# Start addresses of TensorE's operands in SBUF: all tiles moved to multiples of 256 bytes

## The chip, the cores and the metric

The kernel runs on one core of a Trainium2 chip. The metric is device time in microseconds for one execution. Three runs of the kernel before gave 1081.52, 1080.88 and 1080.98 us; the median is 1080.98.

## The reference

One layer of a hybrid decoder: a sequence of 1024 tokens of width 1024, one projection into 6672 columns, two mixers side by side (stick-breaking attention with 16 heads of 64, and a Mamba-2 scan with 16 heads of 64 in chunks of 128), one output projection, a residual with a gate, and a final norm. Everything is in fp32.

```python
mod = silu(c) @ w_ada + b_ada
shift, scale, gate = split(mod, 3)
h = rms_norm(x, norm_in_gain) * (1 + scale) + shift
q, k, v, z_attn, xbc, dt_raw, z_ssm = split(h @ w_in, splits)
o = stick_breaking_attention(q, k, v)
y_attn = rms_norm(o, sb_norm_gain) * silu(z_attn)
xbc = silu(causal_depthwise_conv(xbc, conv_w, conv_b))
y = ssd_scan(xs, softplus(dt_raw + dt_bias), -exp(a_log), b_ssm, c_ssm, d_skip)
y_ssm = rms_norm(y * silu(z_ssm), ssm_norm_gain)
x = x + gate * (concatenate([y_attn, y_ssm]) @ w_out)
return rms_norm(x, norm_f_gain)
```

## The kernel before

**Split products.** A product in fp32 is made of three matmuls in the format fp32r. An operand is split into a high part (hi, the value rounded to fp32r) and a low part (lo, what is left), and hi by hi, hi by lo and lo by hi are added in PSUM; lo by lo is dropped. The normed and modulated input h is kept, transposed, as eight pairs of tiles hh0 to hh7 (hi) and hl0 to hl7 (lo) of 128 x 1024. A piece of w_in is loaded into a raw tile; ScalarE or VectorE makes whi from it, and VectorE subtracts to make wlo (the function split). Most other matmuls (transposes, the values of the attention, the scan) are plain fp32.

A matmul has a stationary operand of 128 x 128, here called the weights, which is loaded ahead of it (LDWEIGHTS, engine PEld in the profile), and a moving operand that is streamed through, here of 512, 384, 272, 256 or 128 columns. In a group of the profile such as pj<-hh,whi the moving tile comes first, the weights second.

**The lines of the split products.** L278 (in mm_f) is the projection with 512 moving columns of hh or hl and the weights whi, wlo: 39 jobs of 48 matmuls. L517 is the same for the first four column blocks, in the first stage. L323, L324 and L327 make the values and dt: there a slice of h is the weights, and whi or wlo are the moving tile, 256 or 272 columns wide. L944 makes the attention scores from q and k. L1101 and L1112 are one more projection job cut in another order. L1047 is the output projection: the weights come from the mixers' results, which are loaded again and split like a piece of w_in, and the moving tile is w_out in hi and lo (woh, wol, and big, bc and be for the second half). L1369 is its last job, with a first part of 512 columns and then two of 256.

**Stages.** Until about 60 us the loads of x, w_ada and the first weights, the modulation, and the first projections (L517). Then the values (L323 and following), the rest of the convolution's columns (L278), the scan (L763 to L777) with projections woven in, and from about 200 us the attention, eight pairs of heads: scores (L944), transposes of the weights (L997), values (L1009), each time with a share of further projections (L278) in between to fill TensorE. After 860 us comes the output projection (L1047), at the end of it alone on TensorE. A table of costs and due times in the code decides at record time what goes between what; from the attention on, the order on each engine is written out by hand.

**Where tiles lie.** SBUF has one address range in each partition; a tile takes the same bytes in all 128. Pools stand one behind the other, in the order in which they are opened: cp (constants), hp (hh and hl), wp (raw, whi, wlo), sp (everything else). In a pool, tiles stand in the order in which their tags are first asked for. Each is padded to 32 bytes. A raw, whi or wlo tile has 544 columns, 2176 bytes, which is 8.5 times 256, so that neighbours differ by 128 in their place within 256 bytes; most others are 4096 or 8192 bytes. The tags raw (two tiles), whi and wlo (four each) are handed out in turn. Every fifth split of the later stages goes to two tiles of tag st instead.

```python
def wtile(dtype, tag):
    return mk(wp, tag, [P, 544], dtype, bufs={"raw": 2, "whi": 4, "wlo": 4}[tag])
```

Of the kernel before, what the change touches and what calls it, by code (L numbers as in the profile page):

```python
# [8 lines left out]
F32 = mybir.dt.float32  # L9
F32R = mybir.dt.float32r  # L10
# [4 lines left out]
P = 128  # L15
S = 1024
D = 1024
KT = 8
TB = 8
HALF = 512  # L20
# [6 lines left out]
def hybrid_layer_kernel(  # L27
# [40 lines left out]
    hp = ctx.enter_context(tc.tile_pool(name="hp", bufs=1))  # L68
    wp = ctx.enter_context(tc.tile_pool(name="wp", bufs=2))
    sp = ctx.enter_context(tc.tile_pool(name="sp", bufs=2))  # L70
    dr = ctx.enter_context(tc.tile_pool(name="dr", bufs=1, space=bass.MemoryType.DRAM))
    pj = ctx.enter_context(tc.tile_pool(name="pj", bufs=2, space=bass.MemoryType.PSUM))
    pz = ctx.enter_context(tc.tile_pool(name="pz", bufs=4, space=bass.MemoryType.PSUM))
# [5 lines left out]
    def mk(pool, tag, shape, dtype=F32, bufs=None):  # L79
        uid[0] += 1  # L80
        kw = {} if bufs is None else {"bufs": bufs}
        return pool.tile(shape, dtype, tag=tag, name=f"{tag}_{uid[0]}", **kw)

    def const(name, shape, dtype=F32):
        return cp.tile(shape, dtype, tag=name, name=name)
# [4 lines left out]
    def duo(dtype=F32):  # L90
        return mk(sp, "be", [P, 2, S], dtype, bufs=4)
# [2 lines left out]
        return mk(pool, tag, [P, HALF])  # L94


    rows = mk(sp, "cbm", [P, 2, P], bufs=2)[:, 0, :]
    pinned[0] = True
    A.dma_start(rows[0:8, :], c.rearrange("o (k p) -> (o k) p", p=P))
# [3 lines left out]
    make_identity(nc, ident)  # L103
    ones = const("ones", [P, P])
    G.memset(ones, 1.0)
    eps_t = const("eps_t", [P, 2])
    G.memset(eps_t[:, 0:1], EPS)
    G.memset(eps_t[:, 1:2], 4.0 * EPS)
    pr = bank(pv, "pv")
# [5 lines left out]
    V.scalar_tensor_tensor(cact, cact, 1.0, cols[:, 0:8], op0=ALU.add, op1=ALU.mult)  # L115
    V.tensor_scalar_mul(cact, cact, 0.5)

    tri = const("tri", [P, P])
    G.affine_select(out=tri, in_=ones, compare_op=ALU.is_ge, fill=0.0, base=0,
                    pattern=[[1, P]], channel_multiplier=-1)  # L120
    late_at = {}
# [57 lines left out]

    h_hi, h_lo = [None] * KT, [None] * KT  # L180

    def wtile(dtype, tag):
        return mk(wp, tag, [P, 544], dtype, bufs={"raw": 2, "whi": 4, "wlo": 4}[tag])

    def split(raw, n, room=None):

        hi, lo = room or (wtile(F32R, "whi")[:, :n], wtile(F32R, "wlo")[:, :n])
        if pinned[0]:
            V.tensor_copy(hi, raw[:, :n])
        else:  # L190
            A.copy(hi, raw[:, :n])
        V.tensor_tensor(lo, raw[:, :n], hi.bitcast(F32), op=ALU.subtract)
        return hi, lo
# [12 lines left out]

    def load_piece(piece, tag="raw"):
        kind, a, g = piece[0], piece[1], piece[2]
        raw = wtile(F32, tag)
        if kind == "f":  # L210
            src = w_in[0][g * HALF:(g + 1) * HALF, a:a + P].rearrange("(k p) f -> p k f", p=P)
            SP.dma_start(raw[:, :HALF].rearrange("p (k f) -> p k f", f=P), src)
        elif kind == "v":
            src = w_in[0][2 * g * P:2 * (g + 1) * P, C_V + a * 256:C_V + (a + 1) * 256]
            SP.dma_start(raw[:, :HALF].rearrange("p (k f) -> p k f", f=256),
                         src.rearrange("(k p) f -> p k f", p=P))
        elif kind == "g":
            SP.dma_start(raw[:, :HALF], w_ada[0][a * P:(a + 1) * P, 2048 + g * HALF:2048 + (g + 1) * HALF])
        elif kind == "b":
            SP.dma_start(raw[0:1, :HALF], b_ada[:, 2048 + g * HALF:2048 + (g + 1) * HALF])  # L220
        else:
            assert piece[3] is u_d or stored == set(range(8))
            src = piece[3][4 * g:4 * g + 4, :, a * P:(a + 1) * P]
            SP.dma_start(raw[:, :HALF].rearrange("p (k t) -> p k t", t=P), src.rearrange("k p t -> p k t"))
        return raw[:, :HALF]
# [72 lines left out]
    def inproj_v(vc, with_dt, v_tiles, dt_raw, extra=None):  # L298

        n = 272 if with_dt else 256  # L300
        wts = {}
        if not with_dt:
            for q, (whi, wlo) in enumerate(take(4)):
                for k in range(2):
                    wts[2 * q + k] = (whi, wlo, slice(k * n, (k + 1) * n))
        else:
            for k0 in range(0, KT, 2):
                raw = wtile(F32, "raw")
                rv = raw[:, :2 * n].rearrange("p (k f) -> p k f", f=n)
                rs = slice(k0 * P, (k0 + 2) * P)  # L310
                SP.dma_start(rv[:, :, :256], w_in[0][rs, C_V + vc * 256:C_V + (vc + 1) * 256]
                             .rearrange("(k p) f -> p k f", p=P))
                SP.dma_start(rv[:, :, 256:272], w_in[0][rs, C_DT:C_DT + 16]
                             .rearrange("(k p) f -> p k f", p=P))
                whi, wlo = split(raw, 2 * n)
                for k in range(2):
                    wts[k0 + k] = (whi, wlo, slice(k * n, (k + 1) * n))
        for i in range(TB):
            ps = bank(pj, "pj")
            ts_ = slice(i * P, (i + 1) * P)  # L320
            for k in range(KT):
                whi, wlo, ws = wts[k]
                K(T.matmul(ps[:, :n], h_hi[k][:, ts_], whi[:, ws], start=(k == 0), stop=False))  # L323
                K(T.matmul(ps[:, :n], h_hi[k][:, ts_], wlo[:, ws], start=False, stop=False))  # L324
                if i == 0 and extra:
                    extra(ps[:, n:n + TB], k)
                K(T.matmul(ps[:, :n], h_lo[k][:, ts_], whi[:, ws], start=False, stop=(k == KT - 1)))  # L327
                if not with_dt:
                    ahead()
                    if i == TB - 1 and k % 2:  # L330
                        used()
                if k == 3:
                    yield 1.4
            if i == 0 and extra:
                extra(ps[:, n:n + TB], KT)
            for j in range(2):
                A.copy(v_tiles[j][:, i * P:(i + 1) * P], ps[:, j * P:(j + 1) * P])
            if with_dt:
                A.copy(dt_raw[:, i, :], ps[:, 256:272])
            yield 1.4  # L340
# [4 lines left out]

    xt = [None] * TB
    ssq = const("ssq", [P, TB])
    rstd = const("rstd", [P, TB])
    shc = const("shc", [P, 8])
    gsc = const("gsc", [P, 8])  # L350
    cact32 = mk(sp, "st", [P, 8, 32], bufs=2)
    V.memset(cact32, 0.0)
    V.tensor_copy(cact32[:, :, 0:1], cact.unsqueeze(2))
# [32 lines left out]

    def load_w4(k):
        if k >= 6:
            w_raw[k] = wtile(F32, "raw")[:, :HALF]
        else:  # L390
            if k % 2 == 0:
                spare.append(mk(sp, "v", [P, 2, HALF], bufs=3))
            w_raw[k] = spare[-1][:, k % 2]
        SP.dma_start(w_raw[k], w_in[0][k * P:(k + 1) * P, C_XBC:C_XBC + HALF])
# [2 lines left out]

    def split_w4(k):
        if k < 4:
            w_hi[k], w_lo[k] = wtile(F32R, "whi")[:, :HALF], wtile(F32R, "wlo")[:, :HALF]  # L400
        else:
            if k == 4:
                w_far["lo"] = duo(F32R)
            if k % 2 == 0:
                w_far["hi"] = mk(sp, "sq", [P, 2, HALF], F32R, bufs=2)
            w_hi[k] = w_far["hi"][:, k % 2]
            w_lo[k] = w_far["lo"][:, k // 2 % 2, k % 2 * HALF:(k % 2 + 1) * HALF]
        A.copy(w_hi[k], w_raw[k])
# [20 lines left out]
    A.activation(rstd[:, 0:1], eps_t[:, 0:1], AF.Sqrt)  # L429

    def norm_x(i):
        junk = mk(sp, "om", [P, 1028], bufs=2)
        A.activation(junk[:, :S], xt[i], AF.Square, accum_out=ssq[:, i:i + 1])
        A.activation(rstd[:, i:i + 1], ssq[:, i:i + 1], AF.Sqrt, scale=1.0 / D, bias=eps_t[:, 0:1])
        V.reciprocal(rstd[:, i:i + 1], rstd[:, i:i + 1])
        V.tensor_scalar_mul(xt[i], xt[i], rstd[:, i:i + 1])
# [88 lines left out]
        A.copy(u[:, 3 + b * HALF:3 + (b + 1) * HALF], ps)  # L525

    def conv_buf(wide=False):
        u = duo().rearrange("p u s -> p (u s)") if wide else mk(sp, "om", [P, 1028], bufs=2)
        G.memset(u[:, 0:3], 0.0)
        return u  # L530

# [49 lines left out]
    for c_ in range(1, 4):  # L581
        k = 2 * c_ - 2
# [129 lines left out]
    def ssd_group(g):  # L712
# [12 lines left out]
        for ch in range(TB):  # L725
# [26 lines left out]
            V.tensor_tensor(xd[:, 0], px.rearrange("p (h r) -> p h r", r=64),  # L752
                            dt_t[:, ch, hs].unsqueeze(2).broadcast_to([P, 8, 64]), op=ALU.mult)
            py = bank(pz, "pz")
            cd = mk(sp, "cdy", [P, 8], bufs=2)
            V.tensor_copy(cd, abc[:, :, P - 1])
            if ch > 0:
                V.tensor_tensor(abc, abc, Ct[:, ts_].unsqueeze(1).broadcast_to([P, 8, P]), op=ALU.mult)
# [46 lines left out]
    def gated(j):  # L805
        if not pinned[0]:
            if j == 0:
                A.activation(sq_s, xs[j], AF.Square)
            else:
                sq = mk(sp, "om", [P, 1028], bufs=2)[:, :S]  # L810
                A.activation(sq, xs[j], AF.Square)
                V.tensor_tensor(sq_s, sq_s, sq, op=ALU.add)
            A.activation(xs[j], xs[j], AF.Copy, scale=cols[:, 100 + j:101 + j])
            SP.dma_start(u_d[j], xs[j])
            return
# [110 lines left out]
    def scores(p, g):  # L926
# [5 lines left out]
        for i in {i for i, _, _ in GROUPS[g]}:  # L932
            if i % 2 == 1:
                tiles[p, i // 2] = [duo(), duo()]
        oms = [mk(sp, "om", [P, 1028], bufs=2), mk(sp, "bc", [P, S], bufs=4)]
        parts = []
        for i, c0, cw_ in GROUPS[g]:
            zs = [bank(pz, "pz") for _ in range(2)]
# [383 lines left out]
    fs = const("fs", [P, TB])  # L1322

    def load_t2(i):
        t2 = mk(sp, "om", [P, 1028], bufs=2)[:, :S]
        SP.dma_start(t2, t2_d[i])
        return t2

# [5 lines left out]
    for i in range(TB):  # L1334
        t2 = t2s[i]
# [21 lines left out]
            after(3.0, finish)  # L1357
            continue

        part = const("part", [P, 3])  # L1360
        yt = take(2)
        cuts = ((0, 512), (512, 768), (768, 1024))
        for n, (c0, c1) in enumerate(cuts):
# [56 lines left out]
```

## Time and profile before

| what | value |
|---|---|
| median of three runs | 1080.98 us |
| the profiled execution | 1080.97 us |
| its span, first to last instruction | 1079.2 us |
| mean granted TensorE clock | 0.999 |
| DVE busy | 767.2 us |
| ACT busy | 536.0 us |
| DMA packets | 91560, 96.15 MB |

A row of the timeline has the start and the length in microseconds, the engine, the line, the operation, the tiles (out<-in, with the weights last), the partitions and columns, and how many equal instructions are merged into the row. A row of the chain has the start and the length of a piece, its engine and line, and the count of instructions in it. A row of the groups has the sum of the busy time and the mean length of one instruction in nanoseconds; the lengths of matmuls overlap, so the spacing of starts is read from the timeline or the chain.

### The profile page before, as it was taken

Reading aid. Unit: us, or ns where it says so; the run is one execution under the profiler, and the core shown is the slowest. Engines: PE = TensorE matmul, PEld = TensorE weight load, DVE = VectorE, ACT = ScalarE, POOL = GpSimd, SP = SyncE. Lnnn points to the kernel's source line nnn. Section 1 sums busy time; section 2 is a strip of 40 time slices with the busy share of each in tenths; the row PEclk is TensorE's granted clock in tenths of the full one; section 3 lists DMA queues with packets and bytes.
Section 4 is the critical chain, followed back from the end, with each engine's and each line's share of the span. In section 5 each row is a group of like instructions: output and inputs, shape, how many; then the busy total and the mean of one; then the engine's idle time right before and its main releaser. Section 6 shows DMA issues by size and latency. Waiting matters only on the chain.

```text
span 1079.2 us, 16251 instructions
## 1 busy us (share of the span) xinstructions
PE 1060.5 (98%) x6323; PEld 836.6 (78%) x6323; DVE 767.2 (71%) x1333; ACT 536.0 (50%) x1163; POOL 3.0 (0%) x23
## 2 busy tenths in 40 slices
PE   7999999999999999999999999999999999999997
PEld 5689877777777877788777887778876777688886
DVE  4737879988838865844977658969387789664554
ACT  5645397656423554644645556546465664420111
POOL 0000000000000000000000000000000000000000
PEclk9999999999999999999999999999999999999999
DMA  9710233233202221101321102311011522555432
GB/s 331 238 41 21 77 107 103 69 99 113 84 20 59 88 69 30 60 20 30 89 68 40 49 21 78 79 39 41 21 50 49 186 90 87 201 182 194 155 107 78
DMA packets 91560, 96.15 MB, mean 89 GB/s; under 512 B 5998, under 2 KB 75994, under 8 KB 91484
## 3 DMA queue, kind: packets, MB, share of 16 engines
q1 hardware_dynamic: 88828, 86.45, 25.6%
q10 hardware_dynamic: 2656, 8.67, 2.4%
q8 instruction: 50, 0.82, 0.3%
q14 instruction: 26, 0.21, 0.1%
HBM read 78.26 MB, written 16.84 MB: 88 GB/s over the span
## 4 chain that ended last, share of the span: by engine, by line
PE 92%; DMA 4%; DVE 2%; ACT 1%; issue 0%; SPq 0%; DVEq 0%; ACTq 0%
PE pj L278 39%; PE pj L1047 15%; PE pt L997 7%; PE pv L1009 6%; PE pz L944 6%; PE pj L323 3%; PE pj L327 3%; PE pj L324 3%; PE pz L517 2%; PE pz L763 1%; PE pv L777 1%; PE pz L768 1%; PE pj L1369 1%; DMA aw<-in_w_ada_dram 1%; DMA big<-in_x_dram 1%; PE pj L1112 1%
## 5 line engine op out<-in xcount | busy, mean ns | idle before, releaser
L278 PE MATMUL pj<-hh,whi 128*128 128x512 f32 x544 | 227.3, 418 | 0.3 <-ACT th L62 0.3
L278 PE MATMUL pj<-hh,wlo 128*128 128x512 f32 x544 | 215.5, 396 | 0.0
L278 PE MATMUL pj<-hl,whi 128*128 128x512 f32 x544 | 214.0, 393 | 0.0
L62 ACT COPY be<-pt 128x512 f32<-128x512 f32 (+1 forms) x192 | 92.5, 482 | 137.3 <-PE pt L997 134.1
L278 PEld LDWEIGHTS pj<-hh,whi 128*128 128x128 f32 x544 | 102.6, 189 | 26.1 <-issue 6.1
L278 PEld LDWEIGHTS pj<-hh,wlo 128*128 128x128 f32 x544 | 102.2, 188 | 24.2 <-issue 0.7
L278 PEld LDWEIGHTS pj<-hl,whi 128*128 128x128 f32 x544 | 102.8, 189 | 17.7 <-issue 0.5
L62 ACT ACTIVATE be<-pz 128x512 f32<-128x512 f32 (+3 forms) x192 | 100.3, 523 | 0.0
L997 PE MATMUL pt<-ident,be 128*128 128x128 f32 x576 | 97.5, 278 | 1.8 <-ACT be L62 1.7
L997 PEld LDWEIGHTS pt<-ident,be 128*128 128x128 f32 x576 | 67.7, 140 | 38.6 <-ACT be L62 28.8
L62 DVE TENSOR_TENSOR wlo<-raw,whi 128x512 fp32r<-128x512 f32 (+1 forms) x109 | 75.4, 693 | 22.9 <-ACT whi L62 16.4
L62 ACT ACTIVATE om<-pz 128x512 f32<-128x512 f32 (+2 forms) x96 | 47.5, 495 | 75.8 <-PE pz L944 75.0
L62 DVE TENSOR_TENSOR_SCAN om<-om,ident 128x128 f32<-128x128 f32 x64 | 26.9, 420 | 66.1 <-ACT om L62 65.9
L62 DVE TENSOR_TENSOR_SCAN om<-om 128x896 f32<-128x896 f32 (+6 forms) x56 | 71.9, 1285 | 2.0
L62 DVE TENSOR_TENSOR_SCAN bc<-bc 128x896 f32<-128x896 f32 (+6 forms) x56 | 71.9, 1285 | 2.0
L1009 PE MATMUL pv<-be,v 128*64 128x256 f32 (+1 forms) x640 | 69.3, 363 | 0.0
L62 DVE TENSOR_TENSOR be<-be,bc 128x1023 f32<-128x1023 f32 (+4 forms) x78 | 65.4, 839 | 2.4
L323 PE MATMUL pj<-whi,hh 128*128 128x256 f32 (+1 forms) x224 | 66.4, 297 | 0.0
L944 PE MATMUL pz<-big,big 64*128 64x384 f32 (+2 forms) x576 | 65.3, 357 | 0.2 <-DVE big L62 0.2
L1009 PEld LDWEIGHTS pv<-be,v 128*64 128x64 f32 x640 | 43.1, 136 | 28.7 <-issue 8.3
L327 PE MATMUL pj<-whi,hl 128*128 128x256 f32 (+1 forms) x224 | 64.3, 287 | 0.0
L324 PE MATMUL pj<-wlo,hh 128*128 128x256 f32 (+1 forms) x224 | 63.4, 283 | 0.0
(287 smaller groups left out, 1992.0 us busy)
## 6 DMA issues: line engine op xcount, KB each, us to landing
raw<-in_w_in_dram SPq DMA_DIRECT2D x98, 256.0 KB, 2.9
be<-acT_d ACTq DMA_DIRECT2D x16, 512.0 KB, 4.1
big<-in_x_dram SPq DMA_DIRECT2D x10, 512.0 KB, 5.7
aw<-in_w_ada_dram SPq DMA_DIRECT2D x16, 256.0 KB, 5.7
u_d<-big SPq DMA_DIRECT2D x8, 512.0 KB, 3.0
y_d<-bc SPq DMA_DIRECT2D x8, 512.0 KB, 2.7
raw<-in_w_ada_dram SPq DMA_DIRECT2D x16, 256.0 KB, 2.7
raw<-u_d SPq DMA_DIRECT2D x16, 256.0 KB, 2.9
```

Source lines behind the costliest of these rows:

```text
L62: return lambda *args, **kw: K(op(*args, **kw))
L278: K(T.matmul(ps, w[:, ws], h[:, b * HALF:(b + 1) * HALF], start=(k == 0 and n == 0), stop=(k == KT - 1 and n == 2)))
L323: K(T.matmul(ps[:, :n], h_hi[k][:, ts_], whi[:, ws], start=(k == 0), stop=False))
L324: K(T.matmul(ps[:, :n], h_hi[k][:, ts_], wlo[:, ws], start=False, stop=False))
L327: K(T.matmul(ps[:, :n], h_lo[k][:, ts_], whi[:, ws], start=False, stop=(k == KT - 1)))
L517: K(T.matmul(acc[f][:, c0:c1], w[:, f * P:(f + 1) * P], h[:, sl], start=(k == 0 and n == 0 and c0 == 0), stop=(k == KT - 1 and n == 2)))
L763: K(T.matmul(po, xd[:, 0, h, :], m[:, h, :], start=True, stop=(ch == 0)))
L768: K(T.matmul(po, st[:, h, :], abc[:, h, :], start=False, stop=True))
L944: K(T.matmul(zs[e][:, :mw], a[r, i * P:(i + 1) * P], k_[r, c0:c0 + mw], start=(n == 0), stop=(n == 2)))
L997: K(T.transpose(ptt[:, (j - j0) * P:(j - j0 + 1) * P], be[:, j * P:(j + 1) * P], ident))
L1009: K(T.matmul(pav[p][64 * e:64 * e + 64, (q0 + u) * P:(q0 + 2) * P], vs[p][:, j * P + 64 * e:j * P + 64 * e + 64], tl[e][:, u:2, j * P:(j + ...
L1047: K(T.matmul(ps, y[:, ks], w(k, b), start=(k == 0 and n == 0), stop=(k == KT - 1 and n == 2)))
```

## The change

Every instruction stays, with the same sizes, in the same order on the same engine and with the same waits; the tiles get other addresses. With each tile's place given as its start modulo 256 bytes:

| tiles | before | after |
|---|---|---|
| hh, hl (and woh, wol, wor in their places) | 192 | 0 |
| whi | 192, 64, 192, 64 | 0, used from 0 |
| wlo | 192, 64, 192, 64 | 128, used from 128 bytes on: 0 |
| wlo when 272 columns are taken twice | as above | 128 and 192 |
| raw | 192, 64 | 0, 128 |
| cbm, st, big, v, bc, be, th | 192 | 0 |
| sq | 0 | 0 |
| om (1028 columns, 4112 bytes) | 192, 224 | 0, 32 |
| ident, ones | 128 | 0 |
| tri | 192 | 0 |

Weights are read in slices of 128 columns, 512 bytes, and moving tiles in slices of a multiple of 128 columns, except the 272-column ones, so a slice keeps its tile's place.

How it is done: four small constants are asked for earlier and one is made larger, so that the constants of 512 bytes stand at 0 and the pool ends at a multiple of 256; whi and wlo get a tag for each of their four tiles, asked for in pairs, so that a whi and its wlo stand side by side, 2176 bytes apart, and the wlo's matrix begins at its 32nd column; the tiles of 4112 bytes and the 32-byte tiles cdy move to a new pool op behind sp. The rotation over four pairs is the same.

```diff
     sp = ctx.enter_context(tc.tile_pool(name="sp", bufs=2))
+    op = ctx.enter_context(tc.tile_pool(name="op", bufs=2))
...
+    eps_t = const("eps_t", [P, 2])
+    rstd = const("rstd", [P, TB])
+    shc = const("shc", [P, 8])
+    gsc = const("gsc", [P, 8])
...
-    eps_t = const("eps_t", [P, 2])
+    tri = const("tri", [P, P])
...
-    def wtile(dtype, tag):
-        return mk(wp, tag, [P, 544], dtype, bufs={"raw": 2, "whi": 4, "wlo": 4}[tag])
+    def wraw(tag="raw"):
+        return mk(wp, tag, [P, 544], bufs=2)
+
+    n_pair = [0]
+
+    def wpair(n):
+
+        i = n_pair[0] % 4
+        n_pair[0] += 1
+        hi, lo = (mk(wp, f"{tag}{i}", [P, 544], F32R, bufs=1) for tag in ("whi", "wlo"))
+        return hi[:, :n], lo[:, 32:32 + n] if n == HALF else lo[:, :n]
 
     def split(raw, n, room=None):
 
-        hi, lo = room or (wtile(F32R, "whi")[:, :n], wtile(F32R, "wlo")[:, :n])
+        hi, lo = room or wpair(n)
...
-            w_hi[k], w_lo[k] = wtile(F32R, "whi")[:, :HALF], wtile(F32R, "wlo")[:, :HALF]
+            w_hi[k], w_lo[k] = wpair(HALF)
...
-        junk = mk(sp, "om", [P, 1028], bufs=2)
+        junk = mk(op, "om", [P, 1028], bufs=2)
...
-            cd = mk(sp, "cdy", [P, 8], bufs=2)
+            cd = mk(op, "cdy", [P, 8], bufs=2)
...
-        part = const("part", [P, 3])
+        part = const("part", [P, 24])
```

More of the change, by code (lines that the diff above doesn't have):

```diff
@@ L116, in hybrid_layer_kernel @@
     V.tensor_scalar_mul(cact, cact, 0.5)
-    tri = const("tri", [P, P])
     G.affine_select(out=tri, in_=ones, compare_op=ALU.is_ge, fill=0.0, base=0,
@@ L208, in load_piece @@
         kind, a, g = piece[0], piece[1], piece[2]
-        raw = wtile(F32, tag)
+        raw = wraw(tag)
         if kind == "f":
@@ L307, in inproj_v @@
             for k0 in range(0, KT, 2):
-                raw = wtile(F32, "raw")
+                raw = wraw()
                 rv = raw[:, :2 * n].rearrange("p (k f) -> p k f", f=n)
@@ L347, in hybrid_layer_kernel @@
     ssq = const("ssq", [P, TB])
-    rstd = const("rstd", [P, TB])
-    shc = const("shc", [P, 8])
-    gsc = const("gsc", [P, 8])
     cact32 = mk(sp, "st", [P, 8, 32], bufs=2)
@@ L388, in load_w4 @@
         if k >= 6:
-            w_raw[k] = wtile(F32, "raw")[:, :HALF]
+            w_raw[k] = wraw()[:, :HALF]
         else:
@@ L527, in conv_buf @@
     def conv_buf(wide=False):
-        u = duo().rearrange("p u s -> p (u s)") if wide else mk(sp, "om", [P, 1028], bufs=2)
+        u = duo().rearrange("p u s -> p (u s)") if wide else mk(op, "om", [P, 1028], bufs=2)
         G.memset(u[:, 0:3], 0.0)
@@ L809, in gated @@
             else:
-                sq = mk(sp, "om", [P, 1028], bufs=2)[:, :S]
+                sq = mk(op, "om", [P, 1028], bufs=2)[:, :S]
                 A.activation(sq, xs[j], AF.Square)
@@ L934, in scores @@
                 tiles[p, i // 2] = [duo(), duo()]
-        oms = [mk(sp, "om", [P, 1028], bufs=2), mk(sp, "bc", [P, S], bufs=4)]
+        oms = [mk(op, "om", [P, 1028], bufs=2), mk(sp, "bc", [P, S], bufs=4)]
         parts = []
@@ L1324, in load_t2 @@
     def load_t2(i):
-        t2 = mk(sp, "om", [P, 1028], bufs=2)[:, :S]
+        t2 = mk(op, "om", [P, 1028], bufs=2)[:, :S]
         SP.dma_start(t2, t2_d[i])
```

## Prediction

> **What bounds the kernel now.** I read the page first (busy shares, then the chain), then the waits of TensorE, then its groups by form, and last the spacing of its matmuls in the chain and the timeline.
>
> ```profile
> PE 1060.5 (98%) x6323; PEld 836.6 (78%) x6323; DVE 767.2 (71%) x1333; ACT 536.0 (50%) x1163; POOL 3.0 (0%) x23
> ...
> PE 92%; DMA 4%; DVE 2%; ACT 1%; issue 0%; SPq 0%; DVEq 0%; ACTq 0%
> ```
>
> TensorE is busy for 98% of the span and carries 92% of the chain that ended last. A busy TensorE need not be one that waits for nobody, so the waits come next.
>
> ```profile
> PE pv L110 <- DMA cbm<-in_norm_in_gain_dram: 5.7, 1, 5.7
> PE pt L997 <- ACT be L62: 1.7, 4, 0.7
> PE pz L763 <- DVE v L62: 1.1, 1, 1.1
> ```
>
> After the first load, the longest entries are 1.7 us and 1.1 us in the whole run. So from about 40 us on the time is a count of matmuls times the spacing between their starts, and nothing else. The recorded length of a matmul (about 390 ns) is not that spacing, since matmuls overlap; pieces of the chain give it, as length by count.
>
> ```profile
> 104.92 23.15 PE pj L278 x100
> ...
> 852.28 7.39 PE pj L1112 x32
> ...
> 949.16 112.08 PE pj L1047 x486
> ```
>
> That is 231.5, 230.9 and 230.6 ns for a matmul with 512 moving columns. The last block of the kernel has the same matmul in two widths:
>
> ```profile
> 1064.28 0.39 PE L1369 MATMUL pj<-be,wlo 128*128 128x512 f32 x1
> ...
> 1066.32 0.39 PE L1369 MATMUL pj<-be,wlo 128*128 128x512 f32 x1
> ...
> 1066.66 0.28 PE L1369 MATMUL pj<-bc,st 128*128 128x256 f32 x1
> ...
> 1069.54 0.28 PE L1369 MATMUL pj<-bc,st 128*128 128x256 f32 x1
> ```
>
> Nine matmuls of 512 columns start within 2.04 us, 226.7 ns each, and 24 of 256 columns within 2.88 us, 120.0 ns each. The difference, 106.7 ns for 256 columns, makes 213.3 ns for the streaming of 512, so each matmul carries a part of 13.3 ns that does not grow with its width. What lies above 226.7 ns elsewhere is the question of this change.
>
> **Does the spacing depend on where a tile starts?** Before, every moving tile of these lines starts 192 bytes past a multiple of 256, and the weight tiles take turns at 192 and 64 past one. In the tail of L1047 one job reads first a weight tile that stands at 64 and then one at 192, twelve matmuls each, and both again for the second half. The rows are the first matmul of each twelve:
>
> ```profile
> 961.38 0.40 PE L1047 MATMUL pj<-woh,whi 128*128 128x512 f32 x1
> ...
> 964.17 0.40 PE L1047 MATMUL pj<-woh,whi 128*128 128x512 f32 x1
> ...
> 966.93 0.40 PE L1047 MATMUL pj<-woh,whi 128*128 128x512 f32 x1
> ...
> 969.73 0.40 PE L1047 MATMUL pj<-woh,whi 128*128 128x512 f32 x1
> ```
>
> 2.79 us and 2.80 us on the tile at 64 (232.5 and 233.3 ns each), 2.76 us on the one at 192 (230.0). A few jobs earlier the weights come from tiles that all stand at 192, job after job:
>
> ```profile
> 951.40 0.39 PE L1047 MATMUL pj<-wol,st 128*128 128x512 f32 x1
> 951.63 0.61 PE L1047 MATMUL pj<-woh,st 128*128 128x512 f32 x2
> 952.08 0.39 PE L1047 MATMUL pj<-wol,st 128*128 128x512 f32 x1
> ```
>
> Three in 0.68 us: 226.7 ns, held for many triples. Same line, same widths, same engines beside it: the spacing does depend on the start, and 226.7 ns is reached where weights and moving tile share one position within 256 bytes and have done so for a while. After a tile at 64 it takes some five matmuls to get back there, which is why a twelve at 192 averages 230.0.
>
> Does a multiple of 256 for the weights alone help? The first stage has weights in tiles that already start there (sq) and, between them, weights at 192 (be), all with the moving tile at 192:
>
> ```profile
> 73.82 1.10 PE L517 MATMUL pz<-hh,sq 128*128 128x512 f32 x4
> 74.75 1.08 PE L517 MATMUL pz<-hh,be 128*128 128x512 f32 x4
> 75.67 1.09 PE L517 MATMUL pz<-hl,sq 128*128 128x512 f32 x4
> 76.61 0.40 PE L517 MATMUL pz<-hh,sq 128*128 128x512 f32 x1
> ```
>
> From sq 0.93 and 0.94 us for four (232.5 and 235.0 ns), from be 0.92 us (230.0). So it is not the multiple of 256 by itself that is good; equal positions do better. After the change both are at 0.
>
> **The change part by part.** No instruction is added, removed or moved on any engine or queue; only addresses differ. So each part is a spacing times a count.
>
> (a) The 512-column matmuls of the split products. By the loops there are 1872 of L278, 720 of L1047 and 240 of L517, L1101, L1112 and L1369: 2832. Not all can gain, since many follow or precede a change of kind.
>
> ```profile
> L278 PE MATMUL pj<-hh,whi 128*128 128x512 f32 x544 | 227.3, 418 | 0.3 <-ACT th L62 0.3
> ...
> L278 PE MATMUL pj<-hl,whi 128*128 128x512 f32 x544 | 214.0, 393 | 0.0
> ...
> L1047 PE MATMUL pj<-woh,whi 128*128 128x512 f32 x92 | 38.9, 423 | 0.0
> ...
> L1047 PE MATMUL pj<-wol,whi 128*128 128x512 f32 x92 | 36.1, 392 | 0.0
> ...
> 104.67 0.48 PE L278 MATMUL pj<-hh,wlo 128*128 128x512 f32 x1
> ```
>
> The first of a triple has 25 ns more than the second in L278 and 31 ns in L1047; one behind a break shows 0.48 us instead of 0.39, 0.09 more. That makes 25 x 544 / 90 = 151 breaks in L278, 32 in L1047, and I allow 15 for the rest. I leave out two matmuls for each break: 1570, 656 and 210 remain. At 226.7 ns instead of 231.5, 230.6 and (from the L517 rows, about 232) 232, they save 1570 x 4.8 = 7.5 us, 656 x 3.9 = 2.6 us and 210 x 5.3 = 1.1 us: **11.2 us**. Bounds: nothing below 213.3 ns can come of it, so at most 28.6 + 11.3 + 3.9 = 43.8 us; and if all ran as on the tile at 64 (233), 2.4 + 1.6 + 0.2 = 4.2 us would be lost.
>
> A rule speaks against this term. The Trainium skill, in "TensorE: Matmul & The Clock Gate", section "Step-by-step: what each phase is for", says that weights and moving operand have independent read ports, so that loading the next weights takes no read bandwidth from the running matmul; by it no start could matter and term (a) would be 0. The 233 against 226.7 ns above disagree with that as far as they go.
>
> (b) The 256- and 272-column matmuls of L323 to L327 and L1369 (816) and the pairs of L944 (576).
>
> ```profile
> 13.16 0.97 PEld L468 LDWEIGHTS pj<-ones,th 128*128 128x128 f32 x8 [0.20 <-issue]
> ...
> L323 PE MATMUL pj<-whi,hh 128*128 128x256 f32 x160 | 47.9, 299 | 0.0
> ...
> L324 PE MATMUL pj<-wlo,hh 128*128 128x256 f32 x160 | 44.9, 281 | 0.0
> ```
>
> Here the moving tiles are those at 64 and 192, and the weights at 192; whi and wlo of both kinds share these rows, and I see no separate pace for them: L324's 281 ns is no longer than the 0.28 us of L1369, where all stand at 192. L944 has both operands at 192 already. I take 0. Bounds: eight weight loads in 0.97 us of which 0.19 is the last one's own length, about 111 ns each, are a floor for the narrow ones: 816 x (120.0 - 111) = 7.3 us; for L944 at most the 13.3 ns on 288 pairs, 3.8 us; above, the same sizes as a loss of 4.2 us in (a) would scale to, some 1.5 us.
>
> (c) Plain fp32 matmuls (transposes, values, scan products). The transposes' moving tile, the identity, goes from 128 to 0.
>
> ```profile
> L997 PE MATMUL pt<-ident,be 128*128 128x128 f32 x576 | 97.5, 278 | 1.8 <-ACT be L62 1.7
> ```
>
> Its 278 ns at 128 is also what the narrow split products show with everything at 192 (0.28 us), so no price is visible. Taken as 0; the rows are rounded to a nanosecond, and one nanosecond on the some 2,500 plain records is 2.5 us on each side.
>
> (d) DVE and ACT on moved tiles. om goes from 192 and 224 to 0 and 32. Their work is covered: TensorE's waits for both engines sum to under 6 us. Without that cover a slower scan would show as waits at L997. Taken as 0.
>
> (e) The start, led by loads.
>
> ```profile
> 7.26 6.67 DMA big<-in_x_dram
> 13.95 6.49 DMA aw<-in_w_ada_dram
> 20.45 7.38 DMA bc<-in_w_ada_dram
> 27.85 5.86 DMA be<-in_w_ada_dram
> ```
>
> These and their neighbours lead the chain for some 38 us; they now land on multiples of 256. Loads of one size into the raw tiles, at 64 and at 192, land after 2.9 us from one source and 2.7 us from another, a spread of 7%, so I put 2.7 us on each side and take 0.
>
> ```profile
> raw<-in_w_in_dram SPq DMA_DIRECT2D x98, 256.0 KB, 2.9
> ...
> raw<-in_w_ada_dram SPq DMA_DIRECT2D x16, 256.0 KB, 2.7
> ```
>
> The sum is 11.2 us off. The profiled execution took 1080.97 us around its span of 1079.2, and the median of the runs is 1080.98, so either base gives 1069.8; I say **1070**.
>
> **The rivals.**
>
> *Absolute alignment.* The fixed 13.3 ns itself could come from starting inside a 256-byte piece and vanish when both start on one. Price: up to the bounds above, 43.8 + 7.3 + 3.8 = 54.9 us, so 1026 at the utmost; half of it gives 1053. For it: the 13.3 ns is there in every row with everything at 192. Against it: weights from sq on a multiple of 256 are no faster, and the rows above never show it smaller in any position.
>
> *Equal positions are bad when both are 0.* Loads of the next weights start with the running matmul; if what decides is which piece both read first, position 0 may be where they meet, and the sq rows are the nearest case: 232.5 to 235.0 ns. At 233 the loss is 4.2 us, **1085**; at 235.0 it is 1570 x 3.5 + 656 x 4.4 + 210 x 3 = 9.0 us, **1090**. It decides as soon as the settled spacing exceeds 231 ns.
>
> *No change.* The 192 and 64 could differ for a reason that the change keeps, for instance the distance between the two copies of a weight tile (hi and lo still lie 2176 bytes or more apart), or the change may only move where the slow matmuls fall. That gives 1081, within 2 us. This is also what the skill's rule in (a) gives.
>
> **How the numbers follow.** Equal positions with the settled 226.7 ns: 0.45, 1063 to 1077 (the low side from (c) and (e), the high side if short runs between breaks never settle). Absolute alignment, in part or whole: 0.22, 1026 to 1063. No change: 0.13. Slower: 0.20, 1083 to 1100. The range 1036 to 1086 leaves out about 0.05 below and 0.09 above. A measurement of this kernel tells about 0.2%, 2.2 us, from no change. Faster has the first two cases, 0.67; same 0.13; slower 0.20.
>
> **What would show it.** Right: the chain's long pieces of L1047 and the tail at 226 to 228 ns a matmul, in the first twelve of a job as in the second, the narrow ones of the last block still at 120.0, and the whole difference in TensorE's stretches after 60 us. The absolute case shows in the last block: under 226.7 and under 120.0 ns. The slower case shows 231 ns or more in the same pieces. Wrong in another way: the waits of TensorE grow, or the start up to 60 us changes by more than 3 us.

## The result, and the profile after

The changed kernel took 1072.78 us, the median of four runs (1072.48 to 1073.49), against 1080.99 for the kernel before (1080.88 to 1081.52). The ratio is 0.9923, with a 95% interval of 0.9908 to 0.9938: 8.2 us or about 0.8% faster, beyond the 0.2% that a measurement tells apart. The forecast was 1070. The profiled execution took 1072.53 us, with a span of 1070.8.

From the page of the changed kernel, the busy times and the shares of the chain that ended last:

```profile
PE 1052.9 (98%) x6323; PEld 836.3 (78%) x6323; DVE 766.2 (72%) x1333; ACT 535.6 (50%) x1163; POOL 2.9 (0%) x23
...
PE 96%; ACT 1%; DMA 1%; DVE 1%; issue 0%; SPq 0%; DVEq 0%; ACTq 0%
```

The counts are those of before, and TensorE's busy time fell by 7.6 us. In the chain TensorE has 96% instead of 92%, and the loads 1% instead of 4%: they lead at the very start only. The waits of TensorE, changed kernel (sum, times, longest, in us):

```profile
PE pv L116 <- DMA cbm<-in_norm_in_gain_dram: 5.6, 1, 5.6
PE pt L1008 <- ACT be L62: 1.6, 3, 0.7
...
PE pz L774 <- DVE v L62: 0.5, 1, 0.5
```

The first two are as before. The third stood at 1.1 us in L763 (now L774), so the waits didn't grow: all of them sum to 10.9 us against 11.6. The pieces of the chain that answer to those of before (lines are shifted: L278 is now L292, L1047 is L1058, L1112 is L1123, L1369 is L1380):

```profile
42.38 7.64 PE pz L528 x33
...
102.50 22.70 PE pj L292 x100
...
315.00 15.18 PE pj L292 x66
...
846.02 7.27 PE pj L1123 x32
...
942.49 110.33 PE pj L1058 x486
...
1052.82 11.20 PE pj L1380 x72
```

The two long pieces run at 227.0 ns for a matmul, where they ran at 231.5 and 230.6. One more piece of before makes the starts comparable along the run:

```profile
320.19 15.45 PE pj L278 x66
```

| mark | before, us | after, us | difference |
|---|---|---|---|
| piece of 100 begins | 104.92 | 102.50 | -2.42 |
| piece of 66 begins | 320.19 | 315.00 | -5.19 |
| piece of 486 begins | 949.16 | 942.49 | -6.67 |
| span | 1079.2 | 1070.8 | -8.4 |

So the gain grows along the run, but more than a quarter of it is there after 102 us, where few split products have run. The last matmul of the first stage's line (before L517, after L528) starts at 79.66 us before and at 77.53 after: 2.1 us are won by then.

Now the tail of the output projection. The changed kernel's timeline, each row twelve matmuls behind the one above it:

```profile
954.74 0.39 PE L1058 MATMUL pj<-woh,whi 128*128 128x512 f32 x1
...
957.46 0.39 PE L1058 MATMUL pj<-woh,whi 128*128 128x512 f32 x1
...
960.18 0.39 PE L1058 MATMUL pj<-woh,whi 128*128 128x512 f32 x1
...
962.90 0.39 PE L1058 MATMUL pj<-woh,whi 128*128 128x512 f32 x1
...
965.62 0.39 PE L1058 MATMUL pj<-woh,whi 128*128 128x512 f32 x1
```

2.72 us for every twelve, 226.7 ns each, the first twelve of a job like the second; before it was 2.79 and 2.76 in turn. The first stage, same view:

```profile
71.79 1.07 PE L528 MATMUL pz<-hh,sq 128*128 128x512 f32 x4
72.69 1.07 PE L528 MATMUL pz<-hh,be 128*128 128x512 f32 x4
73.60 1.07 PE L528 MATMUL pz<-hl,sq 128*128 128x512 f32 x4
74.51 0.39 PE L528 MATMUL pz<-hh,sq 128*128 128x512 f32 x1
```

0.90 to 0.91 us for four, from sq and from be alike. The tiles sq start at a multiple of 256 in both kernels; only the moving tiles came to them. Weights from sq were slower than those from be before (0.93 and 0.94 us against 0.92); now they are level. The last block's narrow matmuls:

```profile
1059.53 0.28 PE L1380 MATMUL pj<-be,whi 128*128 128x256 f32 x1
...
1062.41 0.28 PE L1380 MATMUL pj<-be,whi 128*128 128x256 f32 x1
```

24 in 2.88 us, 120.0 ns each, as before.

And short pieces of the chain. Before:

```profile
454.94 5.74 PE pj L278 x24
461.12 0.70 PE pj L278 x3
```

After:

```profile
448.98 5.67 PE pj L292 x24
455.09 0.70 PE pj L292 x3
```

A piece of 24 gained 0.07 us, 2.9 ns for a matmul; the piece of 100 gained 4.5 ns for each; a piece of three gained nothing. That is the first sign of where the forecast was too large.

### The profile page after: what moved, and what is told of

Its sections match the earlier page's. It is cut to its first block, busy times and chain, and to the rows that moved or that the text cites. A ratio compares the mean times of both kernels' runs of the same rounds, so it can differ in the third digit from the quotient of the medians.

```text
span 1070.8 us, 16251 instructions
## 1 busy us (share of the span) xinstructions
PE 1052.9 (98%) x6323; PEld 836.3 (78%) x6323; DVE 766.2 (72%) x1333; ACT 535.6 (50%) x1163; POOL 2.9 (0%) x23
## 4 chain that ended last, share of the span: by engine, by line
PE 96%; ACT 1%; DMA 1%; DVE 1%; issue 0%; SPq 0%; DVEq 0%; ACTq 0%
PE pj L292 41%; PE pj L1058 15%; PE pt L1008 7%; PE pv L1020 6%; PE pz L955 6%; PE pz L528 4%; PE pj L337 3%; PE pj L341 3%; PE pj L338 3%; PE pz L774 2%; PE pv L788 1%; PE pz L779 1%; PE pj L1380 1%; PE pz L761 1%; PE pj L1123 1%; PE pz L1058 1%
## 5 line engine op out<-in xcount | busy, mean ns | idle before, releaser
L292 PE MATMUL pj<-hh,whi 128*128 128x512 f32 x544 | 225.9, 415 | 0.3 <-ACT th L62 0.3
L292 PE MATMUL pj<-hh,wlo 128*128 128x512 f32 x544 | 214.5, 394 | 0.0
L292 PE MATMUL pj<-hl,whi 128*128 128x512 f32 x544 | 212.7, 391 | 0.0
L292 PEld LDWEIGHTS pj<-hh,whi 128*128 128x128 f32 x544 | 102.5, 188 | 25.3 <-issue 6.3
L292 PEld LDWEIGHTS pj<-hh,wlo 128*128 128x128 f32 x544 | 102.1, 188 | 22.9 <-issue 0.7
L292 PEld LDWEIGHTS pj<-hl,whi 128*128 128x128 f32 x544 | 102.7, 189 | 16.8 <-issue 0.5
```

Source lines behind the costliest of these rows:

```text
L292: K(T.matmul(ps, w[:, ws], h[:, b * HALF:(b + 1) * HALF], start=(k == 0 and n == 0), stop=(k == KT - 1 and n == 2)))
```

## The experiments

The theory is the prediction's: weights and moving tile at one place within 256 bytes settle at 226.7 ns, whichever place it is. Beside it stand absolute alignment (the multiple of 256 is what counts), and, once the start had come out 2 us shorter, a second cause for that part: where the loads land. In all of them the kernel before was run beside the others on the same chip; its median was 1080.55 for the first four, 1080.5 for the next three and 1080.6 for the last three.

**1. The kernel before, 64 bytes further on.** One constant of 64 bytes is put ahead of all tiles. Moving tiles are then at 0 and the weights take turns at 0 and 128. So the moving tiles, and the tiles in which most of the first loads land, stand at multiples of 256, and half the pairs are unequal as before.

```diff
+    const("shift", [P, 16])
```

> The kernel before with 64 bytes more in the constants' pool, so that all moving tiles start at 0 of 256 and the weight tiles alternate between 0 and 128 instead of 192 and 64. Equal positions (the spacing is good where weights and moving tile start at the same place within 256 bytes, wherever that is): nothing of the relation changes, long pieces of L1047 stay at 230 to 231 ns, 1079 to 1081 us. Multiples of 256 (each operand for itself): all moving tiles and half the weights are right, about half the gain, 1076 to 1078. Moving tile alone: the whole gain, 1072 to 1074, 227 ns. If loads landing on multiples of 256 make the start shorter, the last matmul of L517 starts at about 78 us instead of 79.7.

It took 1079.05 us, ratio 0.9985 (0.9976 to 0.9994). Its chain:

```profile
103.03 23.15 PE pj L279 x100
...
946.85 112.08 PE pj L1048 x486
```

The pieces are as long as before to the last digit. What was won, 1.5 us, is won ahead of the first: it begins 1.89 us earlier than before.

**2. The changed kernel, 64 bytes further on.** The same constant; weights and moving tiles are all at 64.

> The changed kernel with 64 bytes more in the constants' pool: every operand of the split products starts 64 past a multiple of 256, moving and weights alike. Equal positions: 1072 to 1073.5 us, long pieces of L1047 at 227 ns. Multiples of 256, or the moving tile alone: the gain is lost, 1080 to 1082 us, 230 ns or more. If the loads' landing place shortens the start, the last matmul of L517 starts at 78.5 to 79.7 us instead of 77.5.

It took 1074.97 us, ratio 0.9947 (0.9931 to 0.9964), 1.5 us above the range expected for equal positions. Its chain:

```profile
104.87 22.70 PE pj L293 x100
...
945.07 110.33 PE pj L1059 x486
```

The pieces are those of the changed kernel, at 64 instead of 0, and the first begins as late as before (104.92). So absolute alignment falls for the matmuls, while the start follows it: what was missed is the early start.

**3. The pairing alone.** Only wpair is put into the kernel before: every whi and wlo is then read from 192, the place of the moving tiles. The moving tiles, the constants, sq and om stay where they were.

```diff
+    def wpair(n):
...
+        hi, lo = (mk(wp, f"{tag}{i}", [P, 544], F32R, bufs=1) for tag in ("whi", "wlo"))
+        return hi[:, :n], lo[:, 32:32 + n] if n == HALF else lo[:, :n]
```

> The kernel before with the pairing of whi and wlo alone: all weights at 192 like the moving tiles, nothing else moved (sq stays at 0, so 64 matmuls of L517 have unequal places). Equal positions: almost the whole gain, 1073.5 to 1075.5 us, L1047 at 227 ns. Multiples of 256, or the moving tile alone: no gain, 1080 to 1082. The start up to the last matmul of L517 stays at 79 to 79.7 us if it is the loads or the sq weights that made it shorter.

It took 1074.59 us, ratio 0.9944 (0.9929 to 0.9959). Its chain:

```profile
104.33 22.71 PE pj L287 x100
...
944.73 110.28 PE pj L1056 x486
```

A third place, 192, and the same pace. The pairing without moving anything to a multiple of 256 gives 6.0 us. With experiment 1's 1.5 us that is 7.5 of the 8.2.

**4. The changed kernel with wlo used from its first byte.** The wlo tiles, the weights of one matmul in three, are then at 128, and all else is as in the changed kernel.

```diff
-        return hi[:, :n], lo[:, 32:32 + n] if n == HALF else lo[:, :n]
+        return hi[:, :n], lo[:, :n]
```

> The changed kernel with wlo used from its first byte, so that of each three matmuls of a split product one reads weights 128 bytes off the moving tile's place and two read them at the same place. Equal positions: the spacing never settles, L1047 at 229 to 232 ns, 1077 to 1081 us. Multiples of 256 for each operand: two thirds of the weights' share stays, about 1074 to 1076. Moving tile alone: unchanged, 1072 to 1074 us, 227 ns.

It took 1078.36 us, ratio 0.9984 (0.9974 to 0.9993): this one line carries most of the change. Its chain:

```profile
102.59 23.14 PE pj L292 x100
...
946.60 112.02 PE pj L1058 x486
```

The early start stays (102.59 against the changed kernel's 102.50) and the pace is that of before.

**5 and 6. Other distances.** Moving tiles stay at 0; the weights go to 32, 160, 64 and 192 in turn, and in the other kernel to 96 and 224. The weight pool goes behind sp, so that its size moves nothing else but om and cdy, whose pool follows it.

```diff
+        if n_pair[0] <= 4 and (8, 0, 8, 0)[i]:
+            mk(wp, f"gap{i}", [P, (8, 0, 8, 0)[i]], F32R, bufs=1)
...
+        a = (0, 32, 0, 32)[i]
+        return hi[:, a:a + n], lo[:, 32 - a:32 - a + n]
```

In the second the numbers are (24, 0, 0, 0).

> The changed kernel with the pool of the weight tiles behind the others and its four pairs at 32, 160, 64 and 192 bytes past a multiple of 256, moving tiles at 0. Equal positions modulo 256: no pair settles at 226.7 ns, each run of twelve at 229 to 236, whole time 1077 to 1082 us (the start stays short). If only the place within 64 or 128 bytes counted, the pairs at 64 and 192 (or 160 and 32 alike) would settle at 226.7. If there is an offset at which the two reads never meet, one of the pairs goes below 226.7 ns, towards the 213.3 of the streaming alone.

> The same with the pairs at 96 and 224 past a multiple of 256. Equal positions: 229 to 236 ns in each run of twelve, 1077 to 1082 us. An offset that avoids the meeting: below 226.7 ns in its runs.

Each ran once: 1080.59 and 1082.50 us, the second 0.5 above its range, though both have the early start. The long piece of the output projection in the chain of experiment 5:

```profile
948.12 112.75 PE pj L1063 x486
```

And of experiment 6:

```profile
949.88 112.94 PE pj L1063 x486
```

232.0 and 232.4 ns, more than before (230.6), since before half of the rotating weights were at the moving tile's place and here none is. (The st tiles still are, which keeps these below 233.) Joining every matmul's start with the addresses of its two tiles gives the mean spacing from the sixth matmul of an unbroken stretch on, by how far the weights lie behind the moving tile within 256 bytes:

| distance, bytes | 32 | 64 | 96 | 128 | 160 | 192 | 224 |
|---|---|---|---|---|---|---|---|
| spacing, ns | 233.4 | 233.0 | 233.9 | 233.1 | 233.1 | 230.3 | 233.1 |

At distance 0 the changed kernel's long stretches have 226.7. Here all weights of a twelve stand at one place, so it is not enough that they agree among themselves. For 512 columns no distance is better than 0.

For 256 columns it is the other way round. The last block of experiment 6, where whi and wlo stand at 96:

```profile
1072.46 0.28 PE L1385 MATMUL pj<-be,whi 128*128 128x256 f32 x1
...
1073.75 0.28 PE L1385 MATMUL pj<-be,wlo 128*128 128x256 f32 x1
```

The twelfth starts 1.29 us after the first, 117.3 ns each, and in experiment 5 the mean at distance 32 is 118.3; equal places have 120.0. So at distance 96 the wide matmul is 7.2 ns slower and the narrow one 2.7 ns faster, and the split into streaming and a fixed 13.3 ns holds for equal places only.

**7. Everything at 128.** In the changed kernel a constant is made 80 bytes shorter and another 84 (64 each after padding), which brings the tiles behind the constants from 0 to 128.

```diff
-    cols = const("cols", [P, P])
+    cols = const("cols", [P, 108])
...
-        part = const("part", [P, 24])
+        part = const("part", [P, 3])
```

> The changed kernel with 128 bytes less in the constants' pool, so that every tile from hh on, the loads' landing places and the weights stand 128 past a multiple of 256. Equal positions: all of TensorE's gain, L1047 at 227 ns, stages behind 80 us as in the changed kernel. The start tells what the loads want: if multiples of 128 do, packets of 1 KB take 46 ns and the last matmul of L517 starts at 77.5 us, 1072 to 1073 us in all; if it takes multiples of 256, 50 ns and 79 to 80 us, 1074 to 1075.

It took 1074.46 us, ratio 0.9945 (0.9928 to 0.9962). Its chain:

```profile
104.17 22.69 PE pj L292 x100
...
944.33 110.33 PE pj L1058 x486
```

The pace of equal places for a fourth place, and the late start. So for the loads 128 is no better than 64 or 192. The loads can be seen in the stretch from 20 to 42 us (its length, then busy time and count of PE, PEld, DVE, ACT and POOL, TensorE's clock, the DMA share, GB/s). Before:

```profile
20.00:42.00 22.00, 20.82 (x127) 14.75 (x123) 15.84 (x32) 10.84 (x18) 0.00 (x0) 1.00 0.93 297
```

The changed kernel:

```profile
20.00:42.00 22.00, 20.93 (x135) 15.54 (x128) 16.68 (x32) 11.68 (x20) 0.00 (x0) 1.00 0.94 330
```

Experiment 1:

```profile
20.00:42.00 22.00, 20.92 (x137) 15.72 (x129) 16.53 (x32) 12.03 (x21) 0.00 (x0) 1.00 0.93 333
```

Experiment 3:

```profile
20.00:42.00 22.00, 20.93 (x130) 14.91 (x130) 16.54 (x32) 10.80 (x18) 0.00 (x0) 1.00 0.94 304
```

Experiment 7:

```profile
20.00:42.00 22.00, 20.81 (x129) 15.02 (x129) 16.11 (x32) 10.79 (x18) 0.00 (x0) 1.00 0.95 304
```

The DMA engines are busy for 93 to 95% in all five, and they move 330 to 333 GB/s where the tiles start at multiples of 256 and 297 to 304 where they start at 192 or 128. A packet of 1 KB takes 46.3 ns in the changed kernel and 50.1 in the kernel before (the mean over the first 45 us), and the other three fall in with these two: 46.4 in experiment 1, 50.0 and 50.1 in experiments 3 and 7. Experiment 2, at 64, has 50.1. All five kernels load the same tiles.

**8 and 9. Breaks put into the long stretch.** If a stretch has to settle, breaks must take the gain away. In the last seven jobs of the output projection a plain fp32 matmul of 128 columns into an unused bank follows every six split products, in the changed kernel (8) and in the kernel before (9).

```diff
+                if cut and k % 2:
+                    K(T.matmul(cut[0][:, :P], ident, ident, start=True, stop=True))
```

> The changed kernel with one plain 128-column matmul into an unused bank after every six matmuls of the seven last full jobs of L1047 (56 breaks in 336 matmuls). Both theories: about 0.18 us for a break, some 10 us longer than the changed kernel. To be read against the next run, the same in the kernel before. If a run settles only at its sixth matmul, these jobs take the same time in both (their runs of six end before), and L1047 as a whole is shorter here by about 0.5 us only, from the 150 matmuls ahead of the breaks. If every matmul with equal positions gains, it stays near the 2.0 us shorter that it is without the breaks.

> The kernel before with the same 56 breaks. Settling at the sixth: in the jobs with breaks within 0.2 us of the run above, whole time 6.3 to 7 us above it (8.4 less the 1.4 to 2 that the tail no longer gains). Every matmul: the whole 8.4 us above it.

Each ran once: 1086.97 and 1093.32 us, 6.35 apart instead of 8.2. Two breaks in a row, from the timeline of experiment 8:

```profile
1001.01 0.38 PE L1062 MATMUL pt<-ident 128*128 128x128 f32 x2
...
1002.61 0.38 PE L1062 MATMUL pt<-ident 128*128 128x128 f32 x2
```

And of experiment 9:

```profile
1006.93 0.38 PE L1051 MATMUL pt<-ident 128*128 128x128 f32 x2
...
1008.55 0.38 PE L1051 MATMUL pt<-ident 128*128 128x128 f32 x2
```

1.60 us from break to break against 1.62. Over the 336 matmuls with breaks the kernels differ by 0.51 us (89.87 against 90.38), where the same 336 without breaks differ by 1.33 (76.16 against 77.49). So breaks do take most of the gain, but 0.5 us stayed where 0.2 was allowed for. It isn't that stretches of six settle: in experiment 8 the spacings behind the second to the sixth matmul (the last one up to the break) are 229, 233, 236, 224 and 232 ns in nearly all of them, 230.8 by the mean. In experiment 9 the mean is 232.7. So unequal places cost 1.9 ns here before anything has settled. A break costs 13.7 us / 56 = 0.245 us in the changed kernel, more than the 0.18 expected.

**10. om back in its old pool.** In the changed kernel the 1028-column tiles and cdy go back to sp, which puts sq at 64; all else is as in the changed kernel. The om tiles start at 0 and 32 past a multiple of 256 here too, so this run tells what sq's unequal places cost, and nothing of the place of om.

```diff
-        junk = mk(op, "om", [P, 1028], bufs=2)
+        junk = mk(sp, "om", [P, 1028], bufs=2)
```

(and so in the other five places)

> The changed kernel with the 1028-column tiles and cdy back in the pool sp, ahead of sq, so that sq stands at 64 past a multiple of 256 and the 64 matmuls of L517 that have weights there lose their equal positions; everything else stays at 0. Equal positions: 64 matmuls in runs of twelve and more, each by 2 to 5 ns, with their neighbours at most 0.7 us; 1072.5 to 1073.5. If the place of om matters to DVE or ACT on the path: 1075 or more.

It took 1072.90 us, ratio 0.9932 (0.9915 to 0.9948), 0.1 us from the changed kernel. Its chain has one visible trace of it, the piece of the first stage where sq is read:

```profile
42.14 7.80 PE pz L527 x33
```

7.80 us against 7.64 with sq at 0. The new pool as such is worth nothing that can be measured. No kernel of this study beat the changed one.

## Why the prediction was right, and what it mis-sized

**The mechanism held.** Equal positions settle at 226.7 ns, at 0 as at 192; the long pieces of L1047 stood at 227.0, inside the 226 to 228 named; the first twelve of a job came like the second; the narrow ones of the last block stayed at 120.0; the waits didn't grow. Experiments 2, 3 and 7 show the same pace at 64, 192 and 128, experiment 4 shows it lost again by one line.

**Term (a) was mis-sized**: too many matmuls, and each at too high a price. It let 1570 matmuls of L278 gain 4.8 ns each, by leaving out two for each of 151 breaks. The trace has 184 unbroken stretches of L278; 84 of them are three long and 37 six. Counted as spacings from one start to the next, only 979 are the seventh or a later one of their stretch. These went from 230.6 to 227.1 ns, 3.4 us together; the second to the sixth gained next to nothing (231.3 before, 231.1 after). The beginning of the stretch of 100 in the changed kernel shows it, with its first, second, seventh and tenth matmul:

```profile
102.25 0.48 PE L292 MATMUL pj<-hh,wlo 128*128 128x512 f32 x1
102.57 0.39 PE L292 MATMUL pj<-hh,whi 128*128 128x512 f32 x1
...
103.73 0.39 PE L292 MATMUL pj<-hh,wlo 128*128 128x512 f32 x1
...
104.41 0.39 PE L292 MATMUL pj<-hh,wlo 128*128 128x512 f32 x1
```

Five spacings in 1.16 us, 232 ns each, then three in 0.68, 226.7 each. Other stretches need some ten; from the eleventh spacing on the mean is 226.7 against 230.7 before, 4.0 ns apart. L278 gave 3.8 us in all instead of 7.5, and its price per matmul, 4.8, came from the longest piece of the chain. L1047, which is nearly one stretch, gave 2.0 us of its 2.6. The prediction had seen that a stretch needs some five matmuls, and named short stretches that never settle as the high side of its times; it then counted two.

**Term (e), taken as 0, was some 2 us**, within the 2.7 put on each side: the loads land sooner at multiples of 256. The two rows from which the 0 was argued couldn't show it, since they compare two sources, and both land at 64 and 192 in turn, which are equally slow (50.1 ns a packet in the kernel before and in experiment 2). Experiment 1 shows the start alone (1.5 us by the medians, 1.89 at the piece of 100), experiment 3 the pairing alone (6.0), and together they make 7.5 of 8.2. In the trace of experiment 3 the gain by lines is 3.7 us for L278, 2.1 for L1047 and 0.4 for the other lines of term (a), less 0.2 in the value lines, 6.0 together. So the forecast's 11.2 us was a 6 for the matmuls, and 1070 is as near to 1072.8 as it is because 2 us came from a part that it had at nothing. That much is luck: by the matmuls alone it would have missed by 5 us instead of 2.8. The claim that the whole difference would lie behind 60 us was wrong by the same amount; the matmul that starts at 50.35 us before starts at 48.47 after.

A rule bears on this. The Trainium skill, in "DMA: Bandwidth & Descriptors", section "How a descriptor splits into AXI transactions", says that a transaction carries up to 256 bytes and has to start at a multiple of 256, and that a transfer which starts elsewhere begins its first one at the multiple below, where it fetches bytes that it doesn't use. It speaks of reading; if it holds for the landing side, a row of 1 KB at 192, 64 or 128 is by estimate five pieces instead of four. The runs agree in the condition (128 is as slow as 64 and 192), while 50.1 against 46.3 ns is 8% more and not a quarter.

**Terms (b), (c) and (d) at 0** stood, nearly. For (b), the narrow matmuls of the last block kept 120.0 ns, but those of the values (L323 to L327) lost 0.2 us by equal places, a mean of 119.4 ns instead of 118.1 where they had stood 128 apart. For (d), TensorE's waits for DVE and ACT sum to 5.3 us against 5.9, so what moved there stayed covered; no run moved om alone. For (c), where the prediction counted some 2,500 plain records and the trace has 2,051, the transposes kept their 278 ns, as the changed kernel's group (sum, mean of one) has it:

```profile
L1008 PE MATMUL pt<-ident,be 128*128 128x128 f32 x576 | 97.6, 278 | 1.8 <-ACT be L62 1.6
```

**The rivals.** Absolute alignment fell: with equal places the settled spacings, 226.7 ns for the wide matmuls and 120.0 for the narrow ones, are the same at 0, 64, 128 and 192. Equal positions bad at 0 fell with the pace of 226.7 there. No change fell for the matmuls. With it fell, as far as it would make the start of a tile indifferent, the rule of two independent read ports that the prediction cites from the Trainium skill, "TensorE: Matmul & The Clock Gate", section "Step-by-step: what each phase is for".

**Open.** Why equal positions help wide matmuls and not narrow ones, why it takes several matmuls to set in, and what the 13.3 ns are, no run here tells. In experiments 8 and 9 unequal places cost 1.9 ns in stretches of six, while the short stretches of L278 show 0.2; that was not followed further. The spacings at distances 32, 96, 160, 192 and 224 come from one run each. And 0.7 us of the change are not in the sum of experiments 1 and 3, whose intervals together are wider than that.

## What to carry to other kernels

Where TensorE is the bound with wide fp32r matmuls in long unbroken stretches, give the weights and the moving tile the same start within 256 bytes, whichever that is, and look for it in the spacing of starts rather than in recorded lengths. Count the gain by the matmuls that stand seventh or later in their stretch, not by all of a line. Don't count on it for 256 columns, where equal places cost a nanosecond or two here. Where a stage is led by loads, let their tiles start at multiples of 256 bytes, and try the two apart, since one shift of addresses does both at once.

## What was not expected of the hardware

Weights and moving tile 128 bytes apart cost 6.4 ns a matmul of 512 columns (233.1 against 226.7), and so does almost any other distance; 192 costs 3.6. A stretch has to run on for some six to ten matmuls before equal places show. For 256 columns the sign turns: 117.3 ns at distance 96, 120.0 at equal places. Loads into tiles at a multiple of 256 moved 330 GB/s and those at 192 or 128 about 300, at the same busy share of the DMA engines.
